# Two feed-forward down projections as seven streamed products, with their sums formed in the up stage and the modulation rows in the first down stage

## The chip, the core and the metric

The kernel runs on one core of one Trainium2 chip. The metric is the device time of one execution in microseconds (us); the time before is the median of 3 runs. TensorE (PE) multiplies, VectorE (DVE), ScalarE (ACT) and GpSimd (POOL) work on tiles, SyncE (SP) issues most transfers. SBUF is the memory on the core; PSUM banks receive matmuls.

## The reference, cut to what matters

One block of a streaming encoder on x (1 x 1024 tokens x 1024 features). Three sub-layers, each with a modulated norm ahead of it and a gated norm behind it: a feed-forward layer, a mixer (attention beside a recurrent branch), and a second feed-forward layer.

```python
def swiglu(h, w_gu, w_down):
    g, u = jnp.split(h @ w_gu, 2, axis=-1)
    return (jax.nn.silu(g) * u) @ w_down          # w_down: 2816 x 1024
...
def sandwich(x, fn, g_pre, g_post, shift, scale, gate, res_w):
    h = modulate(rmsnorm(x, g_pre), shift, scale)
    y = rmsnorm(fn(h), g_post)
    return x + res_w * gate[:, None, :] * y
...
mod = (c_act @ w_ada[l] + b_ada[l]).reshape(b, N_SUB, 3, D_MODEL)   # shift, scale and gate of the three
```

Everything is float32. The change is in the two products with `w_down` (act, 1024 tokens x 2816, times 2816 x 1024), in what makes ready for them, and in when the rows of `mod` are formed.

## The kernel before, in words

**Split products.** Every float32 operand is split into a rounded high part and the rest (`split`, L135: a cast on ScalarE at L136, a difference on VectorE or GpSimd at L137). A product takes three matmuls: high by high, high by low, low by high. A full matmul is a 128x128 stationary tile by a 128x512 moving one.

**Up stage** (`up_phase`, L664). The 2,816 features are 22 blocks of 128 (NF). A feed-forward stage computes act = silu(g) * u per block, transposed (features on partitions, tokens along), and stores it to `act_d` in device memory. The first blocks are plain; from block `DIRECT[sub]` (4 in the first FFN, 3 in the second) a block is computed by seven products of Strassen-Winograd form instead of eight (`block`, L614; ORDER is 1, 2, 6, 5, 7, 3, 4), 84 matmuls each. The weights of block fb+1 are mixed while block fb runs (`mix`, L581): sums on GpSimd (L588), cast on ScalarE (L600), difference on VectorE (L601). ScalarE and VectorE read the PSUM banks (L620 to L644).

**Down stage** (`down_phase`, L739). The 22 blocks of act and of `w_down` are gone through in seven chunks (CHUNKS). For a chunk, `down_w` (L723) loads whole tiles of 128x1024, act and weights, and splits them (weights on GpSimd, act on VectorE); then for each of 8 token blocks (sb) and 2 halves of the output the chunk's blocks are accumulated in a bank `pd` (L766), which is copied to `yacc` by ScalarE (first chunk, L777) or added to it by VectorE (L779). The last two chunks are done for four token blocks and then for the other four, so that the epilogue of the first four (gate and norm in class `Epilogue`, L338: `put`, `update`, `norm`) lies beside matmuls. The very last token block of the kernel goes through `push_last` (L407).

**Modulation rows.** `ada_acc` (L179) forms one set of 1,024 sums: eight loads of 128x1024 rows of `w_ada`, each multiplied by a column of c_act and added to `acc` on VectorE (L185 the first, L187 the seven others). `ada_cols` (L193) then turns it into columns by small matmuls with ones (L200, tile `pc`), `ada_gate` (L259) into a gate tile by matmuls (L276, tile `pg`). These run as generators in a queue `bgq`, of which `bg(n)` (L287) takes n steps: one per Strassen block of the up stage, one per token block of the down stage's middle chunks, three per step of `rec_out_phase` (L991). `bg_flush` (L296) runs what is left.

**What sets the order.** The two FFNs' instructions are issued in the order in which the Python program writes them, engine by engine; each engine takes its own in that order and waits by semaphores. Tiles are taken in turn from rings: three `raw` buffers, four each of `wh` and `wl`, 22 tiles of 128x1024 called `t4`; six PSUM banks `ps` and two `tr`.

## Time and profile before

| | |
|---|---|
| median of 3 runs | 2277.73 us (2277.55 to 2280.48) |
| the profiled execution, time | 2280.03 us |
| the profiled execution, span of the core | 2278.2 us |
| mean granted TensorE clock | 0.992 |
| busy: PE, DVE, ACT, POOL | 97%, 54%, 42%, 26% |
| matmuls at L766 (both down stages) | 2,112 |
| bytes moved by DMA | 250.30 MB, mean 110 GB/s |

The span is from the first to the last instruction on the core. Busy shares are means over stages of different kind; the stages of this kernel follow one another, so each is read in a window of its own. A matmul's duration overlaps with its neighbours', so its price is read from a long unbroken run of them. The first FFN's down stage runs from 488 to 751 us, the second's from 2027 to 2268 us.

### The profile page before, as it was taken

The page shows a single profiled execution, that of the slowest core. Times are in us where ns is not written, and L with a number is a line of the kernel's source. Part 1 is how long each engine was busy: PE and PEld are TensorE (multiplying, and loading weights), DVE is VectorE, ACT ScalarE, POOL GpSimd, SP SyncE. Part 2 cuts the span into 40 slices and gives each one's busy share as a digit, 9 for nine tenths or more (in the row PEclk, how much of TensorE's full clock was granted, in tenths as well). Part 3 has the DMA queues.
Part 4 walks back from the last instruction along what each step waited for, and adds up shares of the span by engine and source line. Part 5 has one row for each costly group of instructions (what it writes and reads, how often), then busy time and mean ns, then how long its engine had stood idle before and what let it go on. Part 6 is the DMA issues. An engine that isn't in the chain of part 4 may idle for free.

```text
span 2278.2 us, 26296 instructions
## 1 busy us (share of the span) xinstructions
PE 2212.8 (97%) x10227; PEld 1837.7 (81%) x10227; DVE 1230.3 (54%) x1740; ACT 945.8 (42%) x1502; POOL 582.3 (26%) x412
## 2 busy tenths in 40 slices
PE   5999999999999999999999999999999999999998
PEld 3877888888778788888898988887788888888886
DVE  6665554535755677643336666546854444433444
ACT  3543333341213587821147777336433333342121
POOL 3432222222225311000021120006432222222224
PEclk9999999999999999999999999999999999999999
DMA  9322332345653211245312011454322222243223
GB/s 295 103 84 92 110 111 92 111 138 187 189 191 121 77 50 40 66 148 166 111 49 67 25 59 53 157 185 158 97 92 83 83 83 83 82 141 110 93 93 120
DMA packets 217748, 250.30 MB, mean 110 GB/s; under 512 B 10864, under 2 KB 172824, under 8 KB 217624
## 3 DMA queue, kind: packets, MB, share of 16 engines
q1 hardware_dynamic: 217512, 248.60, 34.4%
q8 instruction: 80, 1.31, 0.2%
q14 instruction: 44, 0.36, 0.1%
q10 hardware_dynamic: 112, 0.03, 0.0%
HBM read 203.51 MB, written 48.23 MB: 110 GB/s over the span
## 4 chain that ended last, share of the span: by engine, by line
PE 75%; DVE 6%; ACT 4%; DMA 2%; issue 1%; POOL 1%; DVEq 0%; POOLq 0%; ACTq 0%
PE pd L766 17%; PE pj L435 6%; PE pj L433 6%; PE pj L434 6%; PE psX L610 5%; PE psX L612 5%; PE psX L611 5%; PE pj L1064 4%; PE psZ L610 3%; PE psZ L612 3%; PE psZ L611 3%; PE pv L1111 1%; PE psY L610 1%; PE psY L612 1%; PE psY L611 1%
## 5 line engine op out<-in xcount | busy, mean ns | idle before, releaser
L766 PE MATMUL pd<-dh,ah 128*128 128x512 f32 x1440 | 348.9, 393 | 0.0
L766 PEld LDWEIGHTS pd<-dh,ah 128*128 128x128 f32 x1440 | 273.3, 190 | 57.5 <-POOL dh L137 0.5
L434 PE MATMUL pj<-hl,wh 128*128 128x512 f32 x576 | 227.6, 395 | 5.7 <-DVE hl L316 5.7
L435 PE MATMUL pj<-hh,wl 128*128 128x512 f32 x576 | 227.6, 395 | 4.7 <-DVE wl L137 4.1
L433 PE MATMUL pj<-hh,wh 128*128 128x512 f32 x576 | 230.1, 400 | 0.5 <-ACT wh L136 0.5
L779 DVE TENSOR_TENSOR yacc<-yacc,pd 128x512 f32<-128x512 f32 x190 | 121.9, 683 | 193.4 <-PE pd L766 193.2
L601 DVE TENSOR_TENSOR wm<-raw,wm 128x512 fp32r<-128x512 f32 x152 | 109.6, 724 | 160.5 <-ACT wm L600 160.5
L588 POOL TENSOR_TENSOR raw<-wsum,raw 128x512 f32<-128x512 f32 x37 | 48.1, 1299 | 365.7 <-DVE wm L601 360.4
L136 ACT CAST wh<-raw 128x1024 fp32r<-128x1024 f32 (+1 forms) x86 | 86.8, 1011 | 126.5 <-PE pj L434 52.6
L137 POOL TENSOR_TENSOR wl<-raw,wh 128x1024 fp32r<-128x1024 f32 x25 | 61.2, 2456 | 291.9 <-ACT wh L136 247.4
L434 PEld LDWEIGHTS pj<-hl,wh 128*128 128x128 f32 x576 | 109.8, 191 | 29.7 <-DVE hl L316 7.7
L435 PEld LDWEIGHTS pj<-hh,wl 128*128 128x128 f32 x576 | 109.7, 191 | 29.7 <-DVE wl L137 5.7
L433 PEld LDWEIGHTS pj<-hh,wh 128*128 128x128 f32 x576 | 109.8, 191 | 22.9 <-ACT wh L136 0.8
L137 DVE TENSOR_TENSOR wl<-raw,wh 128x1024 fp32r<-128x1024 f32 (+1 forms) x61 | 73.7, 1211 | 84.7 <-ACT wh L136 84.7
L610 PE MATMUL psX<-hh,wm 128*128 128x512 f32 x296 | 115.6, 391 | 2.8 <-ACT mixes L633 2.8
L610 PE MATMUL psX<-hs,wm 128*128 128x512 f32 x296 | 115.3, 389 | 1.6 <-ACT mixes L626 1.6
L612 PE MATMUL psX<-hh,wm 128*128 128x512 f32 x296 | 115.2, 389 | 0.0
L611 PE MATMUL psX<-hl,wm 128*128 128x512 f32 x296 | 115.2, 389 | 0.0
L612 PE MATMUL psX<-hs,wm 128*128 128x512 f32 x296 | 115.2, 389 | 0.0
L611 PE MATMUL psX<-hs,wm 128*128 128x512 f32 x296 | 115.2, 389 | 0.0
L136 ACT CAST dh<-rawd 128x1024 fp32r<-128x1024 f32 x54 | 56.4, 1052 | 138.8 <-DMA rawd<-in_ffn_w_down_dram 105.5
L1064 PE MATMUL pj<-hh,wh 128*128 128x512 f32 x256 | 102.3, 400 | 0.9 <-DVE gate L277 0.9
(303 smaller groups left out, 5283.9 us busy)
## 6 DMA issues: line engine op xcount, KB each, us to landing
rawa<-in_w_ada_dram SPq DMA_DIRECT2D x56, 512.0 KB, 4.3
raw<-in_ffn_w_gu_dram SPq DMA_DIRECT2D x49, 512.0 KB, 4.3
rawd<-act SPq DMA_DIRECT2D x44, 512.0 KB, 3.6
rawd<-in_ffn_w_down_dram SPq DMA_DIRECT2D x44, 512.0 KB, 4.0
raw<-in_w_in_dram SPq DMA_DIRECT2D x44, 512.0 KB, 3.8
sr<-in_ffn_w_gu_dram SPq DMA_DIRECT2D x39, 512.0 KB, 6.4
act<-act SPq DMA_DIRECT2D x37, 512.0 KB, 4.7
rawa<-in_w_ada_dram SPq DMA_DIRECT2D x32, 256.0 KB, 5.6
```

What stands on the lines that cost most here:

```text
L136: nc.scalar.copy(hi, raw)
L137: (eng or nc.vector).tensor_tensor(lo, raw, hi.bitcast(F32), op=ALU.subtract)
L433: nc.tensor.matmul(dst, wh[:, kk, :], xhk[:, sl], start=first, stop=False)
L434: nc.tensor.matmul(dst, wh[:, kk, :], xlk[:, sl], start=False, stop=False)
L435: nc.tensor.matmul(dst, wl[:, kk, :], xhk[:, sl], start=False, stop=last)
L601: nc.vector.tensor_tensor(t[:, 1], src, t[:, 0].bitcast(F32), op=ALU.subtract)
L610: nc.tensor.matmul(dst, t[:, 0, kk, :], xh, start=first and kk == 0, stop=False, skip_group_check=True)
L611: nc.tensor.matmul(dst, t[:, 0, kk, :], xl, start=False, stop=False, skip_group_check=True)
L612: nc.tensor.matmul(dst, t[:, 1, kk, :], xh, start=False, stop=last and kk == 3, skip_group_check=True)
L766: nc.tensor.matmul(pd[h], a_[:, tk], w_[:, h * 512 : (h + 1) * 512], start=(i == 0 and j == 0), stop=(i == n - 1 and j == 2),)
L779: nc.vector.tensor_tensor(yacc[sb][:, sl], yacc[sb][:, sl], pd[h], op=ALU.add)
L1064: nc.tensor.matmul(d, a[:, k, :], b[k][:, sl], start=k == 0 and i == 0, stop=k == KB - 1 and i == 2)
```

## The change

**Down stages.** Act (tokens by features) and `w_down` are cut into halves each way: features into the even and odd blocks of 11 pairs, tokens and output columns into halves of 512. The product of the two becomes seven products of halves, in the order STREAM = (1, 2, 6, 5, 7, 3, 4), each of 11 pairs by 4 token blocks by 3 split terms. A *unit* is one product's one pair: a half tile of an act operand and one of a weight operand, two transfers into one raw tile and one cast and one difference for both (`Units`). The difference is on VectorE, in a third of the units of products 2, 5 and 7 on GpSimd. Units are fetched three ahead. Products 1, 6, 7 and 4 accumulate on the same four banks, `chain`; products 2, 5 and 3 use four banks of their own and are added to `yacc`. Of product 4, the last, seven units are fetched early, during products 7 and 3, and kept.

**Sums.** Four of the act operands and four of the weight operands are sums or differences of halves. `all_sums` forms them in the up stage, one GpSimd instruction per product of a block: four per pair and operand, 88 per FFN. Weights and the first act blocks are loaded for it, later act pairs are taken as they are made. Results are stored to `act_s` and `down_s` from ScalarE's DMA queue, two steps after the last sum of a pair.

**Modulation rows.** In the first FFN only gate 0 and column sets 3 and 4 are left in the queue, and they run in products 1, 2 and 6 of the down stage, one step per unit, through `t4` tiles; what is left is flushed at the end of product 6. Sets 6 and 7 go to `rec_out_phase`, with eight steps per output block instead of three. The mixer's constants are spread over the up blocks.

**Epilogue.** The first four token blocks' `put`, `update` and `norm` stand behind the first four units of product 4, all four token blocks at a time; then the kept units are gone through token block by token block. `push_last` takes only one half of the output from a bank.

```diff
-CHUNKS = (2, 4, 3, 3, 3, 4, 3)
+KEPT_FROM = 4
...
     def ada_acc(v, alloc):
...
+            if raw_home[0] == "t4":
+                raw = t4("rawa")
+            else:
+                raw = wpool.tile([P, 1024], F32, tag="raw", bufs=3, name=nm("rawa"))
             nc.sync.dma_start(raw, w_ada[k * P : (k + 1) * P, v * D : (v + 1) * D])
+            yield None
...
-    def bg(n=1):
+    def bg(n=1, banks=True):
         for _ in range(n):
-            while bgq:
+            while bgq and (banks or at[0] is not BANK):
...
                 def after(i):
                     mix(fb + 1, i)
-                    if fb == NF - 1 and i in ORDER[3:]:
-                        down_w(0, ORDER[3:].index(i))
+                    next(jobs, None)
+                    if i == 3:
+                        next(early, None)
+                    if fb == NF - 1 and i in ORDER[4:]:
+                        units.fetch(ORDER[4:].index(i) + 1)
...
-                bg(1)
...
+            def step(hurry=False):
+                nonlocal n
+                n += 1
+                while ending and (hurry or ending[0][0] + 2 <= n):
+                    _, dst, j, tiles = ending.pop(0)
+                    for k in range(2):
+                        nc.scalar.dma_start(rows(dst, 2 * j + k), tiles[k])
+                if todo and not loaded and not ending:
+                    loaded.append((*todo[0], *pair_load(*todo.pop(0))))
...
+                for o, p, q, op in pair_steps(*job):
+                    nc.gpsimd.tensor_tensor(o, p, q, op=op)
+                    step()
+                    yield
...
+                self.order = [(p, j) for p in STREAM for j in range(PAIRS)]
+
+                last, self.order = self.order[-PAIRS:], self.order[:-PAIRS]
+                for n, unit in enumerate(last[KEPT_FROM:]):
+                    self.order.insert(len(self.order) - 2 * PAIRS + 2 + n * 2, unit)
+                self.order += last[:KEPT_FROM]
...
+                    raw = wpool.tile([P, 2, 512], F32, tag="raw", bufs=3, name=nm("rawd"))
+                    for o, (t, k, half) in enumerate((act_of[p], down_of[p])):
+                        nc.sync.dma_start(raw[:, o], rows(t, 2 * j + k)[:, (h1, h2)[half]])
...
+                    split(raw, hi, lo, nc.gpsimd if p in (2, 5, 7) and j % 3 == 2 else nc.vector)
...
+            for p in STREAM[:-1]:
+                own = p in (1, 6, 7)
+                dst = chain if own else [bank("pv") for _ in range(4)]
+                for j in range(PAIRS):
+                    ops = units.take(p, j, 3)
+                    for i in range(half):
+                        mm(dst[i], i, ops, j == 0 and p not in (6, 7), j == PAIRS - 1)
+                    next(jobs, None)
+                    bg(1, own)
+                if p == 2:
+                    for _ in jobs:
+                        pass
+                if p == 6:
+                    bg_flush()
...
+                for op, sb0, sl in reads[p]:
+                    for i in range(half):
+                        op(sb0 + i, sl, dst[i])
...
-            specs["x", b] = partial(prep_cols, w_in, C_XR + b * P, spare=b == 0)
+            specs["x", b] = partial(prep_cols, w_in, C_XR + b * P)
...
+            bg(4)
             pr = proj(wts["ro", n], rec_h, rec_l)
...
-            bg(3)
+            bg(4)
...
-        bgq.extend([mixer_constants(), ada_cols(6), ada_cols(7), ada_gate(0, 0.5), ada_cols(3), ada_cols(4)])
+        bgq.extend([ada_gate(0, 0.5), ada_cols(3), ada_cols(4)])
...
-        bgq.extend([ada_gate(1, 1.0), ada_gate(2, 0.5)])
+        bgq.extend([ada_cols(6), ada_cols(7), ada_gate(1, 1.0), ada_gate(2, 0.5)])
```

**Where instructions come to stand.** Three places. In the rows, a name's number tells one buffer from the next; L137 (now L143) is the difference of `split`, L187 (now L200) a modulation product, `rawd` and `dh` belong to the down stage. First, VectorE in the first FFN's down stage, where the last set of modulation columns ends, before:

```order
L187 SCALAR_TENSOR_TENSOR acc_4540<-rawa_4696,c_act,acc_4540 128x1024
L779 TENSOR_TENSOR yacc_3701<-yacc_3701,pd_4699 128x512
L779 TENSOR_TENSOR yacc_3701<-yacc_3701,pd_4700 128x512
L187 SCALAR_TENSOR_TENSOR acc_4540<-rawa_4727,c_act,acc_4540 128x1024
L779 TENSOR_TENSOR yacc_3724<-yacc_3724,pd_4730 128x512
L779 TENSOR_TENSOR yacc_3724<-yacc_3724,pd_4731 128x512
L137 TENSOR_TENSOR ah_4755<-rawd_4752,ah_4754 128x1024
L187 SCALAR_TENSOR_TENSOR acc_4540<-rawa_4758,c_act,acc_4540 128x1024
L779 TENSOR_TENSOR yacc_3747<-yacc_3747,pd_4761 128x512
L779 TENSOR_TENSOR yacc_3747<-yacc_3747,pd_4762 128x512
L209 TENSOR_TENSOR adat_4798<-pc_4789,colsA 128x8
L210 SCALAR_TENSOR_TENSOR acol_82<-adat_4798,colsA 128x8
```

The products of a set (acc_4540) stand one by one between the sums of the output. The same place in the changed kernel, VectorE at the end of product 6, and then TensorE there (L863 are the streamed products, L214 a turning):

```order
L143 TENSOR_TENSOR dh_4385<-rawd_4381,dh_4384 128x1024
L200 SCALAR_TENSOR_TENSOR acc_4224<-rawa_4379,c_act,acc_4224 128x1024
L220 TENSOR_TENSOR scol_85<-pc_4420,colsA 128x8
L198 TENSOR_SCALAR acc_4430<-rawa_4431,c_act 128x1024
L200 SCALAR_TENSOR_TENSOR acc_4430<-rawa_4434,c_act,acc_4430 128x1024
L200 SCALAR_TENSOR_TENSOR acc_4430<-rawa_4437,c_act,acc_4430 128x1024
...
L200 SCALAR_TENSOR_TENSOR acc_4430<-rawa_4449,c_act,acc_4430 128x1024
L200 SCALAR_TENSOR_TENSOR acc_4430<-rawa_4452,c_act,acc_4430 128x1024
L223 TENSOR_TENSOR adat_4464<-pc_4455,colsA 128x8
L224 SCALAR_TENSOR_TENSOR acol_82<-adat_4464,colsA 128x8
L143 TENSOR_TENSOR dh_4479<-rawd_4475,dh_4478 128x1024
```

```order
L863 MATMUL px_3698<-dh_4340 128x512
L863 MATMUL px_3698<-dh_4341,dh_4340 128x512
L863 MATMUL px_3698<-dh_4340,dh_4341 128x512
L214 MATMUL pc_4420<-ones_r,acc_4224 128x1 x8
L214 MATMUL pc_4455<-ones_r,acc_4430 128x1 x8
L863 MATMUL pv_4471<-dh_4362 128x512
L863 MATMUL pv_4471<-dh_4363,dh_4362 128x512
```

All eight products of acc_4430 now stand behind scol_85, which waits for the turning pc_4420, and ahead of the next differences; TensorE's first matmul of product 5 stands behind both turnings.

Second, GpSimd in the up stage of the first FFN, before, a block's four sums after the other's:

```order
L588 TENSOR_TENSOR wsum_1140<-sr_1120 128x512
L588 TENSOR_TENSOR sr_1120<-raw_1118,sr_1120 128x512
L588 TENSOR_TENSOR raw_1118<-wsum_1140,raw_1118 128x512
L588 TENSOR_TENSOR raw_1118<-raw_1118 128x512
L588 TENSOR_TENSOR wsum_1277<-sr_1251 128x512
L588 TENSOR_TENSOR sr_1251<-raw_1249,sr_1251 128x512
L588 TENSOR_TENSOR raw_1249<-wsum_1277,raw_1249 128x512
L588 TENSOR_TENSOR raw_1249<-raw_1249 128x512
```

and in the changed kernel (L608 was L588; L814 are the sums for the down stage, in place):

```order
L608 TENSOR_TENSOR raw_1120<-wsum_1142,raw_1120 128x512
L608 TENSOR_TENSOR raw_1120<-raw_1120 128x512
L814 TENSOR_TENSOR top_1148<-top_1148 128x512
L814 TENSOR_TENSOR top_1148<-bot_1149,top_1148 128x512
L814 TENSOR_TENSOR bot_1149<-bot_1149,top_1148 128x512
L814 TENSOR_TENSOR bot_1149<-bot_1149 128x512
L814 TENSOR_TENSOR top_1188<-top_1188 128x512
L608 TENSOR_TENSOR wsum_1292<-sr_1272 128x512
L608 TENSOR_TENSOR sr_1272<-raw_1270,sr_1272 128x512
L814 TENSOR_TENSOR top_1188<-bot_1189,top_1188 128x512
L814 TENSOR_TENSOR bot_1189<-bot_1189,top_1188 128x512
L608 TENSOR_TENSOR raw_1270<-wsum_1292,raw_1270 128x512
```

The sums of the next block's weights (wsum_1292) now stand behind five of the others.

Third, ScalarE in the same blocks, before:

```order
L626 COPY mixes_1260<-psX_1262 128x512
L600 CAST wm_1280<-raw_1249 128x512
L630 ACTIVATE act_1259<-mixes_1260 128x512
L600 CAST wm_1297<-raw_1249 128x512
L633 COPY mixes_1260<-psX_1262 128x512
L600 CAST wm_1314<-raw_1249 128x512
```

and in the changed kernel:

```order
L646 COPY mixes_1275<-psX_1277 128x512
L620 CAST wm_1295<-raw_1270 128x512
L796 DMA downs_118<-top_1148 128x1024
L796 DMA downs_118<-bot_1149 128x1024
L650 ACTIVATE act_1274<-mixes_1275 128x512
L620 CAST wm_1319<-raw_1270 128x512
L653 COPY mixes_1275<-psX_1277 128x512
L620 CAST wm_1337<-raw_1270 128x512
```

Two stores, which wait for GpSimd's sums of top_1148 and bot_1149, now stand in the row of casts and of readings of banks, one pair in each of these blocks.

## Rows read from the trace of the kernel before

**Rows 1.** The page, busy time, share of the span and instructions of TensorE.

```profile
PE 2212.8 (97%) x10227; PEld 1837.7 (81%) x10227; DVE 1230.3 (54%) x1740; ACT 945.8 (42%) x1502; POOL 582.3 (26%) x412
```

**Rows 2.** Chain of waits, both down stages: start us, us, what, count.

```profile
527.98 1.68 PE pc L200 x16
...
622.68 3.20 PE pc L200 x16
...
666.29 2.52 PE pc L200 x16
...
2030.09 233.65 PE pd L766 x1029
```

**Rows 3.** Windows of single stages.

```profile
core 0: us, PE busy (x) PEld busy (x) DVE busy (x) ACT busy (x) POOL busy (x), PEclk, DMA share, GB/s
228.00:285.00 57.00, 57.00 (x253) 47.22 (x252) 29.68 (x39) 20.46 (x36) 15.90 (x12) 1.00 0.33 111
...
488.00:751.00 263.00, 257.12 (x1140) 212.13 (x1139) 153.19 (x165) 76.40 (x99) 86.03 (x52) 0.97 0.53 170
...
620.00:630.00 10.00, 7.79 (x29) 6.50 (x28) 3.73 (x4) 1.04 (x1) 1.55 (x1) 0.66 0.54 190
...
670.00:680.00 10.00, 10.00 (x36) 8.00 (x36) 2.89 (x4) 2.09 (x2) 2.82 (x2) 0.78 0.29 105
...
640.00:650.00 10.00, 10.00 (x45) 8.27 (x45) 7.56 (x9) 2.10 (x2) 2.77 (x2) 1.00 0.84 263
...
969.00:1026.00 57.00, 57.00 (x253) 47.22 (x252) 24.47 (x22) 13.72 (x17) 2.39 (x1) 1.00 0.48 148
...
2027.00:2268.00 241.00, 239.66 (x1056) 197.67 (x1054) 99.00 (x123) 58.39 (x72) 78.13 (x42) 1.00 0.33 111
```

**Rows 4.** TensorE's waits: line waited for, us in total, times, longest us.

```profile
PE pc L200 <- DVE acc L187: 3.8, 2, 2.2
...
PE pd L766 <- POOL dl L137: 2.7, 2, 1.3
```

**Rows 5.** Single lines: count, duration ns minimum/median/maximum, first and last start us, form.

```profile
L200 PE MATMUL pc<-ones_r,acc x64: 164/250/353, 371.9 to 668.5; 128*128 128x1 f32 x64
...
L185 DVE TENSOR_SCALAR acc<-rawa,c_act x7: 744/747/753, 221.1 to 1056.6; 128x1024 f32<-128x1024 f32 x7
...
L187 DVE SCALAR_TENSOR_TENSOR acc<-rawa,c_act,acc x49: 1273/1283/3415, 240.1 to 1082.6; 128x1024 f32<-128x1024 f32 x49
...
L136 ACT CAST dh<-rawd x54: 1037/1052/1062, 480.5 to 2208.5; 128x1024 fp32r<-128x1024 f32 x54
...
L137 DVE TENSOR_TENSOR ah<-rawd,ah x34: 1212/1219/3299, 494.3 to 2188.8; 128x1024 fp32r<-128x1024 f32 x34
...
L137 POOL TENSOR_TENSOR dh<-rawd,dh x22: 2363/2402/3350, 497.1 to 2180.8; 128x1024 fp32r<-128x1024 f32 x22
```

**Rows 6.** Timeline of VectorE in the tail: start us, us, what.

```profile
2270.72 0.68 DVE L416 TENSOR_TENSOR yacc<-yacc,pd 128x512 f32<-128x512 f32 x1
```

**Rows 7.** DMA issues: count, KB each, median us from issue to landing.

```profile
rawd<-act SPq DMA_DIRECT2D x44, 512.0 KB, 3.6
rawd<-in_ffn_w_down_dram SPq DMA_DIRECT2D x44, 512.0 KB, 4.0
...
sr<-in_ffn_w_gu_dram SPq DMA_DIRECT2D x39, 512.0 KB, 6.4
```

**Rows 8.** Timeline of GpSimd and VectorE where the first FFN's first weights are mixed.

```profile
141.67 1.68 POOL L588 TENSOR_TENSOR wsum<-sr 128x512 f32<-128x512 f32 x1 [1.23 <-DVE wm L601]
143.42 1.59 POOL L588 TENSOR_TENSOR sr<-raw,sr 128x512 f32<-128x512 f32 x1
...
141.51 4.66 DVE L563 TENSOR_TENSOR hl<-bot,hh 128x512 fp32r<-128x512 f32 x4
...
146.69 2.48 DVE L601 TENSOR_TENSOR wm<-raw,wm 128x512 fp32r<-128x512 f32 x4
...
151.99 1.68 DVE L601 TENSOR_TENSOR wm<-raw,wm 128x512 fp32r<-128x512 f32 x1 [0.31 <-ACT wm L600]
```

More of the change, by code (lines that the diff above doesn't have):

```diff
@@ L101, in bank @@
         return ps[0].tile([P, 512], F32, tag="ps", bufs=nbank[0], name=nm(name))
+    tr_home = ["tr"]
     def trbank(name):
+        if tr_home[0] == "ps":
+            return bank(name)
         return ps[0].tile([P, 512], F32, tag="tr", bufs=2, name=nm(name))
@@ L177 @@
     gtile = [None, None, None]
+    raw_home = ["raw"]
+    BANK = "needs a bank"
     def ada_acc(v, alloc):
@@ L739, in down_phase @@
+        units = Units()
         def down_phase(make, ahead):
             epi = Epilogue(sub, xin, xout, EPS, make)
[L741 removed]
             half = SB // 2
[L743 to L752 removed]
@@ new lines, in down_phase, with mm, copy @@
+            tail = make is None
+            def mm(dst, i, ops, first, last):
+                hi, lo = ops
+                tk = slice(i * P, (i + 1) * P)
+                for n, (a_, w_) in enumerate(((hi, hi), (hi, lo), (lo, hi))):
+                    nc.tensor.matmul(
+                        dst, a_[:, 0, tk], w_[:, 1, :], start=first and n == 0, stop=last and n == 2,
+                        skip_group_check=True,
+                    )
+            yacc = {}
+            def copy(sb, sl, src):
+                if sb not in yacc:
+                    yacc[sb] = t4("yacc")
+                nc.scalar.copy(yacc[sb][:, sl], src)
@@ new lines, in down_phase @@
+            p = STREAM[-1]
+            for j in range(KEPT_FROM):
+                ops = units.take(p, j, 3)
+                for i in range(half):
+                    mm(chain[i], i, ops, False, False)
+                if j == 0:
+                    units.fetch(len(units.order))
+                epi.put(j, yacc[j], nc.gpsimd if j % 2 else nc.vector)
+                if j > 0:
+                    epi.update(j - 1)
+                if j > 1:
+                    epi.norm(j - 2)
+                if j == KEPT_FROM - 1:
+                    epi.update(j)
+                    epi.norm(j - 1)
+                    epi.norm(j)
@@ new lines, in down_phase @@
+            last_steps = {4: ((), (), 0), 5: ((4,), (), 3), 6: ((5,), (4,), 5), 7: ((6,), (5,), KB)}
+            for i in range(half):
+                sb = half + i
+                for j in range(KEPT_FROM, PAIRS):
+                    mm(chain[i], i, units.got[p, j], False, j == PAIRS - 1)
+                if tail and i == half - 1:
+                    epi.push_last(sb, yacc[sb], chain[i])
+                    break
+                copy(sb, h1, chain[i])
+                epi.put(sb, yacc[sb])
+                updates, norms, n_out = last_steps[sb]
+                for n in updates:
+                    epi.update(n)
+                for n in norms:
+                    epi.norm(n)
+                if ahead:
+                    ahead.fetch(i + 1)
+                    epi.drain(n_out, on_act=(1, 1))
+                epi.fetch(sb + 1)
```

185 lines of the change are left out of this document (98 added, 87 removed).

## The prediction

> **What bounds the kernel now.** I read the page first: TensorE is busy for 97% of the span [rows 1]. So the question is how many matmuls there are and where TensorE stands still. The chain of waits gives the price of one: 233.65 us for 1,029 matmuls of the second down stage [rows 2], or 0.227 us each (durations of single ones overlap). Then I read the busy time of each engine in windows, stage by stage [rows 3]. Three things are to be seen there. In the up stage TensorE has 57.00 of 57 us while GpSimd has 15.90 and VectorE 29.68: no stall, and room on both. The second down stage loses 1.3 of 241 us. The first one, which carries modulation rows, takes 263 us for the same 1,056 matmuls, which at 0.227 are 239.7: 23.3 us are lost, and around two short stops the clock falls to 0.66 and 0.78, means of stretches in which it is partly at 1.2 and partly at 2.4 GHz. The waits [rows 4] name what ends the stops: the sums of the modulation rows on VectorE.
>
> **The matmuls.** Before, a down stage is 22 feature blocks by 8 token blocks by 2 halves by 3 split terms, 1,056 matmuls. After, it is 7 products by 11 pairs of feature blocks by 4 token blocks by 3, 924, of the same 128x512 shape. Two stages lose 2 x 132 = 264, all on the path: 264 x 0.227 = **-59.9 us**. The sums that the products need go to GpSimd and VectorE and are priced below.
>
> **The modulation rows.** A set of columns ends in a turning, 16 small matmuls [rows 5]: 1.68 us where nothing was waited for, 3.20 and 2.52 us behind the stops [rows 2]. Of the four in the first FFN one lies in the up stage (first at 371.9 us), three in the down stage. These three cost 1.68 + 3.20 + 2.52 and the waits of 3.8 [rows 4], 11.2 us, and the clock in the windows from 620 and 670 us another (0.34 + 0.22) x 10 = 5.6: 16.8 us. After, two sets stay there, and the order of VectorE and TensorE at the end of the third product shows how they end: the eight products of the last set stand in one piece behind the turning of the set before, where each stood between sums of the output. That piece is 0.75 + 7 x 1.28 = 9.7 us [rows 5], and TensorE, whose next matmuls are queued behind the turning, waits for it: 1.7 + 9.8 + 1.7 = 13.2 us. The clock then falls once instead of twice; I take half of the 5.6 us. 16.0 instead of 16.8: **-0.8 us**. The other two sets go to the recurrent output phase, where TensorE has no stop now (57.00 of 57, VectorE 24.47) [rows 3]: two turnings of 1.7 and 1 us of waiting, **+4.4**; the one in the up stage goes, **-1.7**.
>
> **Ends.** Both down stages begin with a wait of 1.3 us for GpSimd's low half of a first weight [rows 4]; now three units, split by VectorE, are fetched in the block before: -2.7. In the tail the addition of each half to its sum drops out, since the Square reads the bank itself; one of them, 0.68 us [rows 6], stood on the end: -0.7. Together **-3.4**. The first half's epilogue now lies within the first four units of the last product, and its fourth block must be normalized when TensorE comes to the transposes, 4 x 2.72 + 2 x 4.77 = 20.4 us later. By the durations of its steps it just fits; 0 to 2 us, I take **+1**.
>
> **Supply of the down stages.** Before, a stage fetched 44 tiles of 512 KB. Now 77 units come, each as two halves of 256 KB, into three raw buffers, and each unit lasts 12 x 0.227 = 2.72 us on TensorE. A raw buffer is taken for landing, cast and difference: 4.0 us [rows 7] + 1.05 + 1.22 [rows 5] = 6.3 us, by three buffers a unit each 2.1 us, which is enough. With the difference on GpSimd (2.4 us) it is 2.5, still enough. It is not enough in the fifth product, where seven units of the last one are fetched between its own: 14 in 19 us, which at 2.1 us are 29.4, less what three prefetched units cover. And 14 units are 7.3 MB, 386 GB/s, where the trace has 263 GB/s at a DMA share of 0.84 [rows 3], some 310 at a full one. Between 0 (the lead covers it) and 10 us a stage; I take 2.5, nearer the lower end, since the last product then finds its units there: **+5**. In the third product loads of modulation rows come beside the units; their lag is covered by the stop above.
>
> **Sums in the up stage.** 88 additions of 128x512 per stage go to GpSimd, 7 in a block for some eleven blocks, beside the 4 that the block's own weights take. At 15.90 / 12 = 1.33 us [rows 3], 11 are 14.6 us of a block of 84 x 0.227 = 19.1; VectorE has 29.68 / 3 = 9.9 us in it. Each fits by itself. But they hinder each other: a VectorE difference took 1.68 us beside a GpSimd sum, where four in a row take 2.48, and GpSimd sums then 1.68 and 1.59 [rows 8]. ScalarE gets two stores in a block, two products behind their sums: were GpSimd later than 5.4 us, ScalarE's casts and its reading of the banks would queue behind the store and TensorE behind those. The bounds are 0 (no stop in the up stage now) and the 31 us of the first rival; I take 2 a stage, **+4**, near the lower end, since the weights are mixed one whole block ahead.
> Beside this stands a rule of the Trainium skill, "SBUF — State Buffer", section "Who interferes with whom": a VectorE instruction with two inputs in SBUF and a GpSimd one that reads SBUF exclude each other for whole instructions. By it a dense block needs 14.6 + 8 x 0.62 = 19.6 us in turn, 0.5 more than it lasts, and over 22 blocks this term would be 11 us instead of 4. The trace agrees in part: 1.68 us fits it, but from 141.5 to 146.2 us GpSimd's 3.27 us and four differences worth 2.48 pass within 4.66 [rows 8], less than in turn.
>
> **Sum.** -59.9 - 0.8 + 4.4 - 1.7 - 3.4 + 1 + 5 + 4 = -51.4. The profiled execution took 2280.03 us, so 2228.6; it lies 2.3 us above the median of 2277.73, so the forecast is **2226 us**.
>
> **Rivals.** *First: VectorE and GpSimd hold each other up in the up stage.* In each of 22 dense blocks one late pair reaches TensorE: 1.68 - 0.62 on VectorE and 1.68 - 1.33 on GpSimd, 1.4 us, 31 us in all. 2226 - 4 + 31 = 2253. For it: the pairs above; VectorE would come to 9.9 + 8 x 1.06 = 18.4 of 19.1 us. Against it: that is still below, and a block ahead. Chance 0.12.
> *Second: loads bound the down stages, and it gets slower.* Three buffers give a unit each (L + 1.05 + 1.22) / 3, L the landing. From L = 5.9 us on TensorE waits; the 59.9 us are eaten when a unit takes 2.72 + 59.9 / 154 = 3.11 us, at L = 7.1. At the 6.4 us of the up stage's side tiles [rows 7] it would be 26 us in place of 5, 2247; at 8 us it would be 108, and 2329, slower than before. Against it: the same tiles land in 3.6 and 4.0 us now, and units of 512 KB in 2.72 us are 193 GB/s, under what the trace has shown. For it: each unit is two transfers, and the first stage has 24 loads of modulation rows beside. Chance 0.10, half of it beyond 7.1.
> A page would make this rival likelier: the Trainium skill, "DMA: Bandwidth & Descriptors", section "Measured (HBM→SBUF, 128 partitions, SWDGE, issued from GpSimd)", asks for 1 MiB or more in a transfer for three quarters of the peak, and the change halves its own to 256 KB. No row here shows such halves in a stream.
> *Third: the piece of 9.7 us is hidden,* VectorE being ahead. Then 16.0 - 3.4 = 12.6 us go, and it is 2214. Against it: in the order the piece stands behind the first turning, and that behind the last matmul of the third product. Chance 0.08.
>
> **How the numbers follow.** The forecast has 0.70. A measurement of this kernel can tell 0.2%, 4.6 us, from no change, so "same" is 2273 to 2282. The forecast, the first and third rival and the milder part of the second lie below that: faster 0.70 + 0.12 + 0.08 + 0.03 = 0.93; same 0.02; slower 0.05. The range: its lower end is the third rival without half of the supply term, 2211; its upper end takes in the milder loads and much of the first rival, 2250. Left out are some 0.07 of the first rival, 0.07 of the second and 0.03 at the bottom.
>
> **What would show it.** Right: 1,848 matmuls in the down stages; up-stage windows at 57.00 of 57; in the first down stage one wait of about 10 us of a turning for VectorE's sum and some us at a lower clock behind it; a second down stage near 924 x 0.227 = 210 us; raw halves landing in less than 5.9 us. Wrong: waits of TensorE for differences or stores in the up stage (first rival), for weights behind landing raw halves through whole products (second), or a gain far under 40 us without one of these.

## The result, and the profile after

The changed kernel takes 2255.24 us (2251.16 to 2258.05, four runs) against 2277.64 of the kernel before: a ratio of 0.990, 95% interval 0.988 to 0.992. It is faster by 22 us, not by the 51 that were forecast, and lies above the range (2211 to 2250). The profiled execution took 2258.05 us with a span of 2256.2, the longest of the four.

The page of the changed kernel, busy time, beside [rows 1]:

```profile
PE 2163.2 (96%) x9963; PEld 1789.3 (79%) x9963; DVE 1327.2 (59%) x1680; ACT 1016.5 (45%) x1567; POOL 786.8 (35%) x554
```

TensorE is busy for 50 us less (2212.8 to 2163.2), but the span is only 22 shorter: it stands still for 93 us instead of 65. Its waits, in us, times, longest us, beside [rows 4]:

```profile
PE pc L214 <- DVE acc L200: 11.3, 1, 11.3
...
PE psX L630 <- ACT mixes L653: 7.3, 3, 4.6
...
PE pt L352 <- DVE yacc L399: 4.3, 2, 3.1
...
PE px L863 <- POOL dh L143: 3.9, 2, 1.9
...
PE pj L452 <- POOL wl L143: 2.2, 1, 2.2
...
PE pv L863 <- DVE dh L143: 1.8, 4, 0.8
...
PE pg L289 <- ACT acch L142: 1.4, 1, 1.4
...
PE pg L289 <- DVE yacc L876: 0.9, 1, 0.9
...
PE pg L290 <- DVE acch L143: 0.6, 1, 0.6
```

The first-weights wait of 2.7 us in [rows 4] is gone, as forecast; a wait of 11.3 us is the longest now, with several small ones beside it. Where the time went is read by stage, from the starts of the first and last matmuls of each stage in TensorE's timeline:

| stage, us | before | change | last set spread (e1) | kept spread (e3) | sums left out (e4) | constants late (e5) | five kept (e12) |
|---|---|---|---|---|---|---|---|
| first up stage, Strassen blocks | 350.3 | 354.5 | 354.6 | 354.7 | 348.0 | 350.3 | 352.5 |
| first down stage | 263.3 | 255.3 | 234.5 | 248.8 | 249.7 | 248.5 | 230.2 |
| mixer, up to the second Strassen blocks | 913.8 | 918.5 | 918.9 | 920.1 | 918.2 | 918.8 | 917.8 |
| second up stage, Strassen blocks | 361.8 | 364.9 | 364.5 | 366.5 | 363.8 | 365.7 | 365.2 |
| second down stage | 240.9 | 214.9 | 215.5 | 211.8 | 216.1 | 215.3 | 210.7 |

A stage whose code is the same differs from kernel to kernel by some us: with the up stage untouched the first one takes 352.6 to 354.7 us (the change, e1, e2, e3, e11), and the first down stage takes 248.5 us in e5 and 249.7 in e7, whose edits lie in the up stage alone, where the change has 255.3 in its profiled execution, the slowest of its four. So a few us in a whole stage are no proof of a cause; a wait or a product that is read at its own place is.

The second down stage does most of what was forecast: 26.0 us less, where 132 matmuls of 0.227 us are 29.9. The first gives back 8.0 of the same 29.9. Without any stop it would take 924 x 0.227 = 209.7 us, so 45.6 are lost there, where 23.6 were lost before. By product, from the timeline: products 1, 2 and 6 take 98.5 us (491.92 to 590.40) instead of 89.9, 8.6 lost, 4.6 of them at the two turnings of the gate, with their waits (524.06 to 527.03 and 561.34 to 562.95); the stop behind product 6 takes 16.7 (to 607.11) and product 5 behind it 32.6 instead of 30.0, 19.3 together; products 7 and 3 take 33.8 and 32.9, 6.7 lost; behind the last product's four units and two token blocks, at 726.73, 20.5 us pass for 42 matmuls worth 9.5, 11.0 lost with the transposes. The windows show the same, columns as in [rows 3]:

```profile
core 0: us, PE busy (x) PEld busy (x) DVE busy (x) ACT busy (x) POOL busy (x), PEclk, DMA share, GB/s
...
590.00:600.00 10.00, 2.27 (x18) 1.86 (x16) 7.78 (x8) 4.04 (x6) 2.34 (x1) 0.78 0.77 270
600.00:610.00 10.00, 6.33 (x23) 5.75 (x24) 5.05 (x6) 0.00 (x0) 0.00 (x0) 0.50 0.20 61
610.00:620.00 10.00, 10.00 (x41) 8.13 (x40) 1.97 (x2) 3.16 (x3) 2.40 (x1) 0.87 0.34 109
...
660.00:670.00 10.00, 7.92 (x34) 5.97 (x33) 4.76 (x4) 4.33 (x5) 2.35 (x1) 1.00 0.70 225
670.00:680.00 10.00, 9.12 (x39) 6.77 (x38) 7.06 (x9) 4.57 (x5) 0.00 (x0) 1.00 0.76 232
...
720.00:730.00 10.00, 7.11 (x33) 5.65 (x31) 4.57 (x5) 4.14 (x9) 8.82 (x10) 1.00 0.63 232
730.00:740.00 10.00, 8.61 (x39) 7.27 (x40) 6.25 (x5) 6.94 (x12) 8.85 (x9) 0.83 0.73 233
```

Between 590 and 610 us TensorE has the stop and runs at 1.2 GHz behind it (0.50); 660 to 670 us is product 7, with the clock at 2.4 GHz and TensorE idle for 2 us; 720 to 740 us is the epilogue. VectorE at the stop (start us, us):

```profile
592.39 0.17 DVE L220 TENSOR_TENSOR scol<-pc,colsA 128x8 f32<-128x8 f32 x1 [2.04 <-PE pc L214]
592.47 1.90 DVE L198 TENSOR_SCALAR acc<-rawa,c_act 128x1024 f32<-128x1024 f32 x1
594.41 9.21 DVE L200 SCALAR_TENSOR_TENSOR acc<-rawa,c_act,acc 128x1024 f32<-128x1024 f32 x7
```

The piece of products is 11.1 us long (592.47 to 603.62) and stands behind the turning, as the order of the instructions had it; 9.7 were forecast; most of the difference is the first, which took 1.90 us instead of 0.75. In the first up stage the largest wait of TensorE is 4.6 us. The timeline there, for VectorE, GpSimd, ScalarE and TensorE in turn:

```profile
242.17 0.17 DVE L972 TENSOR_TENSOR sp_s<-sp_s 128x8 f32<-128x8 f32 x1
242.37 1.15 DVE L973 TENSOR_SCALAR sp_pl<-sp_s 128x8 f32<-128x8 f32 x1
243.55 1.21 DVE L975 TENSOR_TENSOR sp_pl<-sp_pl,sp_s 128x8 f32<-128x8 f32 x1
244.79 0.17 DVE L976 TENSOR_SCALAR sp_pl<-sp_pl 128x8 f32<-128x8 f32 x1
...
242.19 1.30 POOL L608 TENSOR_TENSOR sr<-raw,sr 128x512 f32<-128x512 f32 x1
243.45 1.28 POOL L814 TENSOR_TENSOR top<-bot,top 128x512 f32<-128x512 f32 x1
...
251.36 0.63 ACT L650 ACTIVATE act<-mixes 128x512 f32<-128x512 f32 x1 [9.93 <-DVE mixes L640]
...
252.41 0.58 ACT L653 COPY mixes<-psX 128x512 f32<-128x512 f32 x1
...
253.03 0.79 PE L630 MATMUL psX<-hh,wm 128*128 128x512 f32 x1 [4.59 <-ACT mixes L653]
```

These rows are read backwards: TensorE waits for ScalarE's reading of a bank, ScalarE for VectorE (9.93 us idle), and VectorE stands in the mixer's constants, small instructions on 128x8, of which some take 1.15 to 1.21 us and others 0.17. The long ones end when a sum on GpSimd does: 242.37 + 1.15 and 242.19 + 1.30 are 243.52 and 243.49, 243.55 + 1.21 and 243.45 + 1.28 are 244.76 and 244.73. The kernel before has the same constants in its up stage too, from 200 to 208.25 us, and TensorE waits there as well, but shorter:

```profile
211.24 0.50 PE L610 MATMUL psX<-hh,wm 128*128 128x512 f32 x1 [1.90 <-ACT mixes L633]
```

So of the 4.59 us the change has added 2.7. The sums stretch VectorE's larger instructions too, as the groups of the changed kernel show (count, then busy us and mean ns, then idle us):

```profile
L621 DVE TENSOR_TENSOR wm<-raw,wm 128x512 fp32r<-128x512 f32 x152 | 160.1, 1057 | 166.9 <-ACT wm L620 157.3 <-DMA raw<-in_ffn_w_gu_dram 7.4 <-PE psZ L632 1.8
L814 POOL TENSOR_TENSOR act<-act,act 128x512 f32<-128x512 f32 x54 | 84.6, 1567 | 157.4 <-DMA act<-act 119.0 <-issue 24.5 <-DVE wm L621 11.9
```

The differences of weights took 724 ns before, on average, and 1057 now.

### The profile page after: what moved, and what is told of

Same layout as the page of the kernel before. It is cut to its first block, busy times and chain, and to the rows that moved or that the text cites. A ratio compares the mean times of both kernels' runs of the same rounds, so it can differ in the third digit from the quotient of the medians.

```text
span 2256.2 us, 26782 instructions
## 1 busy us (share of the span) xinstructions
PE 2163.2 (96%) x9963; PEld 1789.3 (79%) x9963; DVE 1327.2 (59%) x1680; ACT 1016.5 (45%) x1567; POOL 786.8 (35%) x554
## 3 DMA queue, kind: packets, MB, share of 16 engines
q8 instruction: 78, 1.28, 0.2%
## 5 line engine op out<-in xcount | busy, mean ns | idle before, releaser
L142 ACT CAST dh<-rawd 128x1024 fp32r<-128x1024 f32 x154 | 161.2, 1052 | 229.8 <-DMA rawd<-downs 86.3
L621 DVE TENSOR_TENSOR wm<-raw,wm 128x512 fp32r<-128x512 f32 x152 | 160.1, 1057 | 166.9 <-ACT wm L620 157.3
L143 DVE TENSOR_TENSOR dh<-rawd,dh 128x1024 fp32r<-128x1024 f32 x122 | 158.5, 1303 | 164.9 <-ACT dh L142 159.3
L450 PE MATMUL pj<-hh,wh 128*128 128x512 f32 x576 | 230.1, 400 | 1.6 <-ACT wh L142 1.0
L863 PE MATMUL px<-dh,dh 128*128 128x512 f32 x592 | 184.6, 393 | 5.5 <-POOL dh L143 3.9
L863 PE MATMUL pv<-dh,dh 128*128 128x512 f32 x528 | 166.5, 397 | 1.9 <-DVE dh L143 1.8
L143 POOL TENSOR_TENSOR wl<-raw,wh 128x1024 fp32r<-128x1024 f32 x25 | 61.5, 2469 | 298.6 <-ACT wh L142 254.1
L814 POOL TENSOR_TENSOR act<-act,act 128x512 f32<-128x512 f32 x54 | 84.6, 1567 | 157.4 <-DMA act<-act 119.0
L863 PE MATMUL px<-dh 128*128 128x512 f32 x352 | 138.7, 394 | 0.4 <-ACT dh L142 0.4
L863 PEld LDWEIGHTS px<-dh,dh 128*128 128x128 f32 x592 | 111.2, 189 | 32.0 <-POOL dh L143 4.9
L143 DVE TENSOR_TENSOR wl<-raw,wh 128x1024 fp32r<-128x1024 f32 (+1 forms) x61 | 77.7, 1274 | 88.9 <-ACT wh L142 88.9
L143 POOL TENSOR_TENSOR dh<-rawd,dh 128x1024 fp32r<-128x1024 f32 x18 | 43.0, 2390 | 246.6 <-ACT dh L142 246.6
L630 PE MATMUL psX<-hh,wm 128*128 128x512 f32 x296 | 116.5, 394 | 7.3 <-ACT mixes L653 7.3
L863 PEld LDWEIGHTS pv<-dh,dh 128*128 128x128 f32 x528 | 100.6, 191 | 25.3 <-DVE dh L143 4.3
L630 PE MATMUL psX<-hs,wm 128*128 128x512 f32 x296 | 115.5, 390 | 1.5 <-ACT mixes L646 1.4
```

The source lines that it names most:

```text
L142: nc.scalar.copy(hi, raw)
L143: (eng or nc.vector).tensor_tensor(lo, raw, hi.bitcast(F32), op=ALU.subtract)
L450: nc.tensor.matmul(dst, wh[:, kk, :], xhk[:, sl], start=first, stop=False)
L621: nc.vector.tensor_tensor(t[:, 1], src, t[:, 0].bitcast(F32), op=ALU.subtract)
L630: nc.tensor.matmul(dst, t[:, 0, kk, :], xh, start=first and kk == 0, stop=False, skip_group_check=True)
L814: nc.gpsimd.tensor_tensor(o, p, q, op=op)
```

## The experiments

Twelve kernels, each compared with the kernel before on the same chip; the numbers by stage and product are from the profile of one execution each.

**e1: the last set of modulation columns spread over product 5.**

```diff
                 if p == 6:
-                    bg_flush()
-                    raw_home[0] = "raw"
+                    while len(bgq) > 1:
+                        bg()
...
+                if p == 5:
+                    bg_flush()
+                    raw_home[0] = "raw"
```

> Edit: at the end of product 6 only the set of columns already summed is turned; the eight products of the last set then run one per unit of product 5 and are turned behind it. Theory (the stop at the end of product 6 is VectorE's piece of eight products, read as 16.7 us from 590.40 to 607.11 us in the changed kernel, and 2.6 us of lower clock behind it): the stop shrinks to one turning of about 1.7 us there and one of 1.7 to 3 us behind product 5, the first down stage falls from 255.3 to about 240 us, the whole by 13 to 16 us. Rival (VectorE or the loads are full in these products, and the stop only moves): the waits for units in product 5 and 7 grow, and less than 5 us are gained.

Measured: 2236.03 us (2234.26 to 2237.44), ratio 0.981 (0.980 to 0.983), 19.2 us under the change; the first down stage 234.5 us. Behind product 6 one turning takes 1.7 us (589.78 to 591.49), one more behind product 5 (621.55 to 623.25), and product 5 itself 30.06 us. TensorE's waits in this kernel's first down stage:

```profile
PE pg L289 <- DVE yacc L876: 2.4, 1, 2.4
PE pj L452 <- POOL wl L143: 2.2, 1, 2.2
PE pt L352 <- DVE yacc L399: 1.8, 2, 1.2
PE px L863 <- POOL dh L143: 1.5, 1, 1.5
PE px L863 <- DVE dh L143: 1.3, 2, 0.8
```

The wait for the sum rows is gone altogether and nothing of its size came in its place: the theory holds. The gain is above the 13 to 16 us that were expected, but at its own place it is not: the stop falls from 16.7 to 1.7 us, product 5 from 32.6 to 30.1, and a turning of 1.7 is added, 15.8 us in all. The other 5 us of the stage lie in places that the edit does not touch. So the piece without a cover cost some 16 us, clock included.

**e2: gate products of the first half on VectorE** (`epi.put(j, yacc[j], nc.vector)`).

> Edit: in the first half's epilogue all four gate products go to VectorE, none to GpSimd. Theory (GpSimd, which takes the small rstd steps one after the other, starts the fourth gate product only at 724.91 us and so delays the fourth block's norm; TensorE waits 3.09 + 1.19 us for it): these two waits fall to under 1.5 us together and the piece from 726.73 to 733.27 us from 6.5 to 3 us or less, the whole by 3 to 6 us with the clock behind it; the second down stage stays. Rival (the chain is bound by the rstd steps themselves, not by the gate product): the wait stays above 3 us.

Measured: 2250.11 us (2246.84 to 2253.74), ratio 0.988 (0.986 to 0.989), which overlaps that of the change. In its trace the wait for the norms falls to 1.8 us (longest 1.2), the piece named falls from 6.5 to 3.4 us, but the next one, with the other half's transposes, grows from 3.2 to 4.8, by a wait of 1.6 for ScalarE's reading. Behind the four units and two blocks 8.5 us are lost instead of 11.0; kernels that left the gate products as they were show 8.6 to 10.4 (e1, e3, e4, e5, e11). In e1, with the gate products still on GpSimd, the piece named takes 3.5 us too. So this run does not show that GpSimd's late gate product makes the loss at the end, and most of that loss is not explained by it.

**e3: kept units one for four others, from product 5 on.**

```diff
-                    self.order.insert(len(self.order) - 2 * PAIRS + 2 + n * 2, unit)
+                    self.order.insert(3 * PAIRS + 2 + n * 5, unit)
```

> Edit: the seven kept units of the last product are fetched one for every four others, from product 5 on, not one for every two in product 7 and the first units of product 3. Theory (units are bound by the time a raw buffer is taken, some 2.2 us a unit with three buffers, so one unit more for two wants 1.81 us): products 7 and 3 lose 3.8 + 2.9 us in the first FFN and 4.5 + 0.9 in the second, all to be gained but 1 to 2 us, 9 to 11 us in all. Rival (VectorE, GpSimd or the sums of the epilogue hold the units, or bandwidth): the waits move to product 5 and the gain is under 4 us.

Measured: 2243.08 us (2239.52 to 2250.74), ratio 0.985 (0.983 to 0.987). Products 7 and 3 take 29.9 and 30.4 us in the first FFN (33.8 and 32.9 before) and 32.0 and 30.4 in the second (34.5 and 30.9). 9.4 us are gained there, as the theory had it. The halves of the stored sums land in 3.7 and 3.8 us (median; 3.6 and 3.7 in the change), those of act and the weights in 3.8 and 4.1 (3.7 and 4.2), so it is how closely the fetches follow each other and not the landing that made the loss.

**e4: the sums' additions left out.**

> Leaves out the 176 additions of the sums on GpSimd; their loads and stores stay, so the stored operands are the plain ones and the output differs. Theory (the additions cost the up stages by holding VectorE's differences and by stores waiting on ScalarE's queue): the up stages fall from 354.5 and 365.4 us to within 1 us of before (350.3 and 362.3), and the first two products of each down stage lose less; 6 to 10 us in all. Rival (the loads and stores themselves, at twice the traffic, delay the weights): the up stages stay at 354 and 365 us.

Measured: 2242.67 us (2240.16 to 2247.01), ratio 0.985 (0.983 to 0.986), 12.6 us under the change. The first up stage falls by 6.5 us, to 2.3 less than before the change, the second only by 1.1, and product 1, up to the gate's turning, takes 30.7 us instead of 33.7 (31.5 to 32.0 in e1, e2, e3 and e5, which keep the additions). The mean difference of weights falls from 1057 to 802 ns, and TensorE's wait behind the mixer's constants from 4.59 to 1.73 us. So the additions, not their loads and stores, cost the first up stage. In the second the theory gets a third of what it expected, and the trace shows what most of the rest is. In the change and in e4 alike, ScalarE stands idle there until a store of sums has landed, and TensorE waits for it, 1.91 us in the change and 1.75 in e4; the row of ScalarE in each, the change first:

```profile
1772.58 0.63 ACT L650 ACTIVATE act<-mixes 128x512 f32<-128x512 f32 x1 [7.25 <-DMA downs<-top]
...
1760.69 0.63 ACT L650 ACTIVATE act<-mixes 128x512 f32<-128x512 f32 x1 [7.09 <-DMA downs<-top]
```

The kernel before has no wait of TensorE over 0.3 us in that stage. So here the rival holds for some 1.9 of 3.1 us: the stores delay it. No run took the stores out to settle it.

**e5: the mixer's constants late** (`if i == 3 and fb >= 15: next(early, None)`).

> Edit: the mixer's constants (27 small VectorE instructions in one piece) are taken from block 15 of the up stage on, where no sums of weights run on GpSimd, not from the first Strassen blocks. Theory (the piece is stretched by the sums beside it, from 0.17 to 1.15 us for some, stands from 237.5 to 248.8 us on VectorE and makes TensorE wait 4.6 us at 253.03 us): that wait goes, the clock beside it too, the first up stage falls from 354.5 to about 349 us, the whole by 4 to 6 us. Rival (the wait comes of the dense blocks themselves, by stores on ScalarE's queue or loads): another wait of some us takes its place in the same stage, less than 2 us are gained.

Measured: 2248.21 us (2246.6 to 2248.99), ratio 0.987 (0.985 to 0.988); the first up stage 350.3 us, 4.3 less than the change and some 2 to 4 less than the kernels that leave the constants where they were. The wait of 4.6 us is gone, and from 250 to 260 us, where the change had TensorE busy for 6.97 us at 0.66 of the clock, it is busy for 10.00 at 1.00. A shorter wait stands where the constants are now:

```profile
457.48 0.50 PE L630 MATMUL psX<-hh,wm 128*128 128x512 f32 x1 [1.67 <-ACT mixes L653]
```

So the theory holds for the stretch by the sums, some 2.9 us and the clock behind it, and not for the wait as a whole: the 27 instructions, most of them one behind the other, make TensorE wait 1.67 us without the sums, as they did in the kernel before (1.90) and in e4 (1.73).

**e6: modulation rows in the up stage again** (`bg(1)` behind each block).

> Edit: one step of the modulation queue per up block as before the change, the rest in the down stage, so that nothing is left to flush behind product 6. Theory (the first down stage's loss is the rows' placing): its 255.3 us fall to 232 to 238 us, as in the run with the last set spread; the up stage rises by 3 to 8 us, for the rows come beside the sums and through the raw buffers of the weights. Rival (the rows cost as much beside the sums): the up stage rises by over 15 us and the whole changes by less than 5.

Measured: 2241.01 us (2238.81 to 2245.15), ratio 0.984 (0.983 to 0.986). The first down stage takes 234.8 us, 20.5 less; the first up stage 358.7, 4.2 more. Both are as the theory had them. With the rows beside the sums the up stage loses some 4 us, and with no piece left to flush behind product 6 the first down stage gains 20.5, although products 1, 2 and 6 still take 99.7 us there. With e1, which keeps all rows in the down stage, this shows that not their being there is the loss but the piece without a cover.

**e7: stores of the sums from SyncE's queue** (`nc.sync.dma_start` in place of `nc.scalar.dma_start`).

> Edit: the stores of the sums go out from SyncE's queue, not ScalarE's. Theory (on ScalarE's queue they mostly wait for nothing, and it is SyncE, which issues every load, that must not wait for GpSimd): the up stages get slower or stay, 0 to +10 us. Rival (the stores hold up ScalarE's casts and readings of banks in dense blocks): the up stages fall by 3 us or more each.

Measured: 2266.74 us (2266.06 to 2267.45), ratio 0.995 (0.993 to 0.997): 11.5 us slower than the change, the first up stage 362.7 us, 8.2 more, the second 370.8, 5.9 more. The theory holds: the placing on ScalarE's queue, which I had counted as a risk, is worth more than 10 us here.

**e8: e1, e2, e3 and e5 together.**

> Edit: the last set spread over product 5, all gate products of the first half on VectorE, kept units one for four, and the mixer's constants late, together. Theory (four separate losses on TensorE): the gains measured alone, 19 and 5 and 12 us, and 4 to 6 expected of the constants, add up but for some 5 us of clock counted twice: 2255 - 35 to 41, 2214 to 2220 us. Rival (they share one cause, and one's gain is another's): over 2228 us.

Measured: 2233.95 us (2232.76 to 2236.75), ratio 0.981 (0.979 to 0.982), only 2 us under e1 alone: a miss. The up stage (350.1 us) and the second down stage (212.2) have their gains, but the first down stage takes 243.9 us, 9.4 more than in e1, and product 5 up to its turning 39.7 instead of 30.1, the last 3.7 of them a wait for VectorE. Its windows there, columns as above:

```profile
598.00:608.00 10.00, 9.97 (x44) 7.91 (x43) 4.55 (x4) 3.16 (x3) 1.86 (x1) 1.00 0.80 282
608.00:618.00 10.00, 6.60 (x27) 5.10 (x28) 7.29 (x7) 3.16 (x3) 2.35 (x1) 1.00 0.71 258
618.00:628.00 10.00, 5.26 (x21) 3.49 (x19) 5.28 (x6) 5.31 (x7) 1.05 (x1) 0.93 0.80 285
```

From 608 to 628 us TensorE is busy for 12 of 20 us, while the DMA moves 258 to 285 GB/s. Kept units and the loads of the last set meet in one product.

**e9: as e8, but kept units one for three, in products 7 and 3 only.**

> Edit: as the four together, but the kept units are fetched one for three others in products 7 and 3 only, so that product 5 has the last modulation set's loads without them. Theory (in the four together, product 5 took 39.7 us instead of 30.1 because kept units and modulation rows, 16 loads more, came in the same product): product 5 takes 30 to 31 us again, products 7 and 3 at most 2 us more than 29.95 each, the first down stage 228 to 233 us, the whole 2220 to 2227 us. Rival (gate products on VectorE or the late constants made it, or the columns' turning): product 5 stays above 35 us and the whole above 2230.

Measured: 2232.09 us (2227.69 to 2236.66), ratio 0.980 (0.978 to 0.982). Product 5 takes 32.8 us, so the meeting was most of what cost e8; products 7 and 3 take 31.2 and 32.7 us in the first FFN and 33.6 and 32.8 in the second, 1 to 4 over, so one for three is still too many. The time is above what was expected.

**e10: e6 with e2, e3 and e5.**

> Edit: one step of the modulation queue per up block (as in the run with the rows in the up stage), the kept units one for four from product 5 on, all gate products of the first half on VectorE, the constants late. Theory (product 5 is then free of modulation rows): product 5 at 30, 7 and 3 at 30 to 32 us in the first FFN; the first down stage 228 to 232 us, the first up stage 350 to 355 us instead of 358.6; the whole 2222 to 2230 us. Rival (rows in the up stage cost there what they give back): the up stage stays above 357 us.

Measured: 2234.99 us, ratio 0.981 (0.979 to 0.983), five runs from 2226.72 to 2240.91, the widest of all: inconclusive as a time. Its profile (of the fastest run) has the first down stage at 232.5 us, half a us over what was expected, the up stage at 352.4, as expected, and the second down stage at 211.2. The time is above what was expected.

**e11: no difference of product 7 on GpSimd** (`p in (2, 5)` in place of `p in (2, 5, 7)`).

> Edit: in product 7 no difference goes to GpSimd (4 of 11 did); nothing else. Theory (in product 7 TensorE waits 1.93 us for GpSimd's difference in both FFNs, since a unit whose raw buffer is taken 2.4 instead of 1.2 us longest holds all behind it): the wait for GpSimd goes, product 7 falls from 33.8 and 34.5 us by 1 to 3 us each. Rival (three raw buffers are too few for three units in the time of two, whoever does the difference): a wait for VectorE's difference of about the same length takes its place and product 7 changes by less than 1 us.

Measured: 2247.54 us (2245.55 to 2249.55), ratio 0.987 (0.985 to 0.988). In the change three of product 7's eleven differences are on GpSimd (j % 3 == 2), not four. Product 7 falls from 33.8 to 31.0 us, within what was expected, and from 34.5 to 30.9, more than that. Its waits in the second down stage

```profile
PE pv L863 <- DVE dh L143: 0.9, 2, 0.5
PE px L863 <- DVE dh L143: 0.4, 1, 0.4
```

are 1.3 us where the change waits 1.9 for GpSimd and 0.7 for others. Most of the loss of product 7 goes here with GpSimd's difference of 2.4 us, and in e3, which keeps it, with the closely fetched units (29.9 and 32.0 us). So the loss needs both.

**e12: e1, e2, e5 and five kept units, one for four, in products 7 and 3; six units of the last product go first.**

```diff
-KEPT_FROM = 4
+KEPT_FROM = 6
...
-                    self.order.insert(len(self.order) - 2 * PAIRS + 2 + n * 2, unit)
+                    self.order.insert(4 * PAIRS + 1 + n * 5, unit)
...
-                if j == 0:
-                    units.fetch(len(units.order))
+                if j >= half:
+                    continue
```

> Edit: the last set spread over product 5, gate products of the first half on VectorE, constants late, and six units instead of four of the last product before the token blocks, so that five units are kept and fetched one for four others in products 7 and 3; the epilogue of the first half has 5.4 us more matmuls over it. Theory (a unit needs some 2.2 us of supply, and the transposes wait because the first half's norms are late): products 7 and 3 take 30 to 31 us in both FFNs, the wait for the fourth block's norm goes, the first down stage takes 226 to 232 us, the second 211 to 213 us; the whole 2216 to 2226 us. Rival (what is left are chance meetings of VectorE and GpSimd which move from run to run): the first down stage stays at 234 to 240 us and the whole within 2228 to 2236.

Measured: 2228.26 us (2227.11 to 2230.26), ratio 0.978 (0.977 to 0.980): the best of all, 27 us under the change. It is 2 us above what was expected, at the lower edge of the rival's range, though the first down stage is as the theory had it and the second 0.3 us better. The first down stage takes 230.2 us, the second 210.7, one over the 209.7 without a stop; products 5, 7 and 3 take 30.0, 30.1 and 29.9 in the first FFN. The longest waits in its first down stage:

```profile
PE pt L352 <- ACT h L341: 3.2, 2, 3.0
PE pj L452 <- POOL wl L143: 2.2, 1, 2.2
PE pg L289 <- DVE yacc L876: 1.0, 1, 1.0
...
PE pt L352 <- DVE yacc L399: 0.6, 1, 0.6
```

The wait for the norms is 0.6 us now, but TensorE waits 3.2 for ScalarE's reading of transposes, and the loss at the end stays 10.9 us: more matmuls over the epilogue did not help it.

## Why the prediction was wrong, by its own steps

Measured against forecast for the profiled execution: 2258.05 and 2228.6, 29.5 us. Some 20.6 of these lie in the first down stage. The count of matmuls and the place of the long stop were right. What failed are the prices of what else stands on TensorE's path: the supply of product 7, the first half's epilogue, the sums in the up stage and the size of the stop were too low, and what products 1, 2 and 6 lose was not in the sum.

- **The matmuls, -59.9:** right. 1,848 are left, and the second down stage shows 26.0 of its 29.9.
- **The modulation rows, -0.8:** the mechanism was right (one stop, a piece of products uncovered behind the turning), the size of the stop was not: 16.0 forecast, 19.3 measured (16.7 and 2.6), of which e1 gains 15.8 by covering the piece, the turnings staying. The clock took 2.6 in product 5 and slowed the second turning, and the piece itself was 11.1 us, not 9.7. The part that moved, +4.4, was right: from the first to the last matmul with the recurrent output's weights 157.4 us pass instead of 153.2.
- **Not in the sum:** products 1, 2 and 6 lose 8.6 us. 4.6 are the gate's two turnings with their waits, which cost 2.2 before (from 577.26 and 582.53 us): I had counted the gate as unchanged, but TensorE waits for its parts now (pg in the list of waits: 1.4, 0.9 and 0.6 us; 0.7 before). The other 4 lie in products 1 and 2. With the additions of the sums out (e4) the three products take 95.5 instead of 98.5 us; but kernels that change nothing there show 94.6 (e5) to 98.4 (e3), so what makes these 4 us stays open.
- **Supply, +5 for both stages:** it was 6.7 in the first alone, 5.5 in the second (34.5 and 30.9 for 29.95 each). I read the order of fetching wrongly: one kept unit is fetched for two others, 21 units in 38 us, not 14 in 19, and it reaches into product 3. At the 2.1 us a unit of my own rows 21 take 44, 6 more than 38, so it was in reach. And I had called GpSimd's 2.5 us a unit still enough; e11 shows that it costs some 3 us a stage when other units are fetched between.
- **The first half's epilogue, +1:** 11.0 lost for 3.2 before, four pieces of transposes of 0.8 us each; 6.8 over the forecast. It did not just fit. The waits name the fourth block's norm (4.3 us in the change), and in e12, where that wait is 0.6, ScalarE's reading of transposes (3.2); e2 does not show that the gate product on GpSimd is the cause, and no run shows what would remove the loss, so it stays open.
- **Ends, -3.4:** both first waits went; the tail did not get shorter, 10.7 us behind the last matmul's start where 10.6 were (8.2 to 11.5 in the other kernels, so 0.7 can't be told there).
- **Sums in the up stage, +4, and the turning gone, -1.7:** 4.2 + 3.1 were measured, so with the turning's 1.7 the sums cost 9.0. In the first stage 2.7 us and a stretch at a lower clock behind them come of the mixer's constants, which made TensorE wait 1.90 us before and 4.59 with the sums beside them; in the second stage 1.9 us are a wait for a store of sums. I had priced neither.
- **Not in the sum either:** among the mixer's first weights TensorE waits 2.2 us for GpSimd's low half, where it waited 0.7 before. The change takes one of these weights out of a spare tile, which may be why; this was not tried alone.

The first rival gave 2253 us, near the result, and is not what happened: VectorE's differences were stretched (1057 ns for 724), but the sums cost TensorE 9.0 us in the two stages, not 31. A time that fits is no proof of its cause; the stages are. My case against a full exclusion of VectorE and GpSimd was weak: the 3.27 us of GpSimd from 141.5 us on contain its own waiting, for two such sums take 2.6 us where nothing holds them, and 2.6 + 2.48 is only 0.4 more than the 4.66 that passed. The second rival fell: the halves land in 3.6 to 4.2 us, as the whole tiles did before (3.6 and 4.0). The third fell in the change, and e1 shows what it would have been.

The rule of the Trainium skill that was weighed there ("SBUF — State Buffer", section "Who interferes with whom") would have made the term 11 us where I took 4 and 9.0 were measured. That is near, but at least 1.9 of the 9.0 are a store. The constants agree with the rule, waiting out a sum of GpSimd (L975, two inputs, 1.21 us), and L973, which has only one tensor as input, was held as long (1.15 us).

Behind the single sizes stands a mistake of method: two unknown costs (supply, sums) were taken near their lower ends, the epilogue's bounds of 0 to 2 us were too narrow, the gate and the constants had no price, and the range was then set by one rival at a time. The misses are of one sign and add up to some 29 us, about as much as the first rival alone.

## What to carry to other kernels

When work is moved under matmuls, look in the order of the instructions for the place where it ends: eight products behind a turning that TensorE waits for cost some 16 us, the same eight one per unit cost nothing that the trace shows. Streamed operands have a price per unit (time a buffer is taken, divided by the buffers), and every extra fetch, every slower engine in that chain must be checked against the matmuls of the very product in which it falls. When several unknown costs are taken near their lower ends, the forecast should be moved by their sum, not only its range.

## What had not been expected of the hardware

Small VectorE instructions on 128x8 took 1.15 to 1.21 us beside GpSimd's sums where they take 0.17 alone, so that a chain of 27 of them and one on GpSimd stood for 11.3 us (237.50 to 248.78); the kernel before shows it already, with 1.25 and 1.09 us beside the sums of its weights (201.97 and 203.49 us). Stores of the sums on ScalarE's queue cost less than on the queue that issues the loads, by 11.5 us (e7); 36 of them land in 3.9 us (median), but one that took 8.1 us held ScalarE for 7.25. And gains measured alone did not add up (e8), since two of them had moved their loads into the same product.
